# A fixed handicap for VectorE in the engine choice of a self-planning decoder kernel

## The chip, the cores and the metric

The kernel runs on one core of one Trainium2 chip. The metric is the time of one execution on the device in microseconds (us), the median of several runs. Engines are named as in the profile: PE is TensorE's matmul side and PEld its weight load, DVE is VectorE, ACT is ScalarE, POOL is GpSimd, and SP is SyncE, which here issues most of the transfers.

## The reference

Two layers of a decoder trunk, 512 tokens of 1024 features, all in float32. Cut to what matters here:

```
for l in range(2):
    u = rms_norm(x, norm_g[l]) * (1 + scale) + shift      # shift, scale, gate = silu(c) @ w_ada[l] + b_ada[l]
    z = u @ w_in[l]                                       # one wide projection, split into the parts below
    ya = dsa_attention(...)      # A: scores of an indexer, top 128 keys of each query, softmax over those
    yb = swa_sinks_attention(...)                         # B: window of 128 keys, with sinks
    yc = stick_breaking_attention(...)                    # C
    merged = sum(sigmoid(m_b) * ((y_b * silu(g_b)) @ w_br_b) for b in (a, b, c))
    x = x + gate * (merged @ w_out[l])
return rms_norm(x, final_g)
```

## The kernel before, in words

**Matmuls in three terms.** Every large product is made of two parts of each operand: a weight chunk that lands in `wstage` is cast to a short form `whi`, and `wlo = wstage - whi` is the rest; activations have `uh` and `ul` in the same way. A product is then `whi*uh + whi*ul + wlo*uh`, three matmuls of 128 x 512. So each chunk of weights (four blocks, 12 matmuls of PE) costs one cast and one subtraction on some other engine (`Chunks.do_split`). There are four buffers each of `wstage`, `whi` and `wlo`, three PSUM banks `ps_z` for projections and five `ps_s` for attention.

**Stages of a layer.** First seven column tiles of the projection that accumulate while the normed input is made (`first_phase`), then the value columns (`v_phase`, tiles of 364 columns). Then several streams are woven together: the indexer and its top-k, mixers C, B and A with four pairs of heads each, the other projection tiles, the branch products that are merged (`branch_item`: `xm <- ps_z, sm` and `sm <- ps_z, sm` take a branch product out of PSUM and multiply it by its gate), and in layer 1 the dot products with `w_ada` that layer 2 needs (`wstage <- wstage, csr`). Last comes the output product (`out_phase`). The top-k runs on VectorE alone: for each of three query blocks 16 times MAX8 and MATCH_REPLACE8 on `score`; mixer A cannot mask its logits before it is done. In mixer C the probabilities `t` are transposed by PE (`ps_s <- small, t`) and copied out to `U`; mixers A and B transpose through VectorE (`X <- X`) and DMA (`U <- X`, `V <- X`).

**A planner sets the order.** Nothing is issued as the Python code runs. `Recorder.add` records each operation with the engines that could do it (`alts`) and a cost on each. `cast` may go to ACT, DVE and, if the source is in SBUF, POOL; `both` (tensor-tensor operations) to POOL and DVE; `sq_` to three engines; a few more have two. `forward` then places one operation after another: for each engine it takes the ready operation that can start first, by urgency (`prio`, the latest start that `latest` found in the round before), and the earliest of the engines' candidates goes. Where an operation has several engines, `elsewhere` decides whether this engine must leave it: it compares when the operation would end here with when it would end on each other engine, from when that engine is free and from the cost there. `order` does five such rounds and keeps the one whose planned end is the earliest; `emit` writes it out. So one changed comparison can change every engine's order. `TOPORT` and `port` in the plan keep VectorE and GpSimd from using a shared SBUF port at once, and `emit` adds a dependency from the VectorE operation to the GpSimd operation that follows it there.

Of the kernel before, what the change touches and what calls it, by code (L numbers as in the profile page):

```python
# [25 lines left out]
F32 = mybir.dt.float32  # L26
F32R = mybir.dt.float32r
BF16 = mybir.dt.bfloat16
AF = mybir.ActivationFunctionType
# [4 lines left out]
P = 128  # L34
# [12 lines left out]
TR32 = {'a': (0, 1, 2, 3), 'b': (0, 1, 2, 3)}  # L47
# [34 lines left out]
class Weave:  # L82


    def __init__(self):
        self.items = []
        self.now = 0.0
        self.events = set()
# [193 lines left out]
class Recorder:  # L282
# [5 lines left out]
    ENTER = {"m": 0.0, "t": 0.035, "c": 0.17, "r": 0.17}  # L288
    TOPORT = 0.13
    ROUNDS = 5  # L290

    def __init__(self, tc, nc, psum, sbuf):
        self.tc, self.nc, self.psum, self.sbuf = tc, nc, psum, sbuf
# [263 lines left out]

    def elsewhere(self, x, name, at, E):

        end = at + x.alts[name].cost  # L560
        for o, y in x.alts.items():
            if o != name:
                t = max(E[o]["free"], x.est, x.soft.get(o, 0.0), E[o]["port"] if y.port else 0.0) + y.cost
                if t < end - 1e-9:
                    return True
        return False

# [28 lines left out]
    def order(self):  # L596
        best = None
        for n in range(self.ROUNDS):
            end, out = self.forward()
# [31 lines left out]
def op(cost, fn, *chunks):  # L631
    return ("op", cost, fn, [c + (phase[0],) for c in chunks])
# [15 lines left out]
def trunk(ctx, tc, xT, vecs, w_ss, w_gt, w_first, w_t, w_v, w_br, w_o, rope, consts, out):  # L648
# [7 lines left out]
    rec = Recorder(tc, nc, ps, sb)  # L656
    PE, ACT, DVE, POOL, SP = (rec.engine(e) for e in ("PE", "ACT", "DVE", "POOL", "SP"))
# [7 lines left out]
    def sbank():  # L665
        return rec.tile("ps_s", [P, S])
# [4 lines left out]
    def t512(tag, bufs=None, dt=F32):  # L671
        return rec.tile(tag, [P, S], dt)

    def mm(o, lhsT, rhs, start, stop=True):
        PE.matmul(o, lhsT, rhs, start=start, stop=stop, skip_group_check=True)
# [24 lines left out]
    def fill(out, v):  # L700
        rec.add({"POOL": ("memset", (out, v), {}), "DVE": ("memset", (out, v), {})})
# [9 lines left out]
    csb, o = small[:, 0:8], 8  # L711
    g_sb = [small[:, o + 8 * l:o + 8 * l + 8] for l in range(L)]
    fg_sb, o = small[:, o + 8 * L:o + 8 * L + 8], o + 8 * L + 8
    b_ada, o = [small[:, o + 24 * l:o + 24 * l + 24] for l in range(L)], o + 24 * L
    sink, o = small[:, o:o + 8 * L], o + 8 * L
# [59 lines left out]
    st = {}  # L775
# [403 lines left out]
    def low_parts(q, kl, pos, banks, b, p, order):  # L1179

        quads = []
        for e, i in order:
            k0, W = keys(b, i)
            bk, c0 = pos(e, i)
            hp = (H0, H1)[e]
            quads.append((banks[bk][:, c0:c0 + W], q[hp, e, 128 * i:128 * i + 128], kl[hp, k0:k0 + W], False))
        value_run(b, RIDE.get((b, p), ()), zbank, quads)
# [3 lines left out]
    def c_qk(p):  # L1191
        def fn():
            q = st[f"cq{p}"]
            kh, kl = st[f"ck{p}"]
            zb, pt = [None] * 5, [None] * 5
            for i in (3, 2, 0, 1):
                ts, W = slice(128 * i, 128 * i + 128), 128 * i + 128
                o, first = [None] * 2, [False] * 2
                for e in range(2):
                    bk, c0 = apos(e, i)  # L1200
                    if zb[bk] is None:
                        zb[bk], first[e] = sbank(), True
                    o[e] = zb[bk][:, c0:c0 + W]
                for e in range(2):
                    mm(o[e], q[:, e, ts], kh[:, e, :W], first[e])
                if i == 1:
                    mm(o[1], q[:, 1, ts], kl[:, S:], False)
            low_parts(q, kl, apos, zb, "c", p, LOW_ALL)
            for bk in (0, 3, 1, 4, 2):
                z = zb[bk]  # L1210
                if bk % 3:
                    m = z[:, 256:].rearrange("p (a b) -> p a b", a=2) if bk != 2 else z.rearrange("p (a b) -> p a b", a=2)[:, :, 128:]
                    DVE.tensor_tensor(out=m, in0=m, in1=cmask.unsqueeze(1).to_broadcast([P, 2, P]), op=OP.add)
                else:
                    DVE.tensor_tensor(out=z[:, 384:], in0=z[:, 384:], in1=cmask, op=OP.add)
                t = pt[bk] = t512("t", 10)
                u32 = mybir.dt.uint32
                rec.add({"ACT": ("activation", (t, z, AF.Abs), {}),
                         "DVE": ("tensor_scalar", (t.bitcast(u32), z.bitcast(u32), 0x7FFFFFFF, None), dict(op0=OP.bitwise_and))})
                ACT.activation(t, t, AF.Exp, scale=-1.0)  # L1220
                ACT.activation(t, t, AF.Ln, bias=1.0)
                DVE.scalar_tensor_tensor(t, z, 0.0, t, op0=OP.min, op1=OP.subtract)
                fill(t[:, 511:512], BIG)
                back = t[:, 0:511][:, ::-1]
                DVE.tensor_tensor_scan(back, z[:, 1:512][:, ::-1], back, BIG, op0=OP.add, op1=OP.subtract)
                ACT.activation(t, t, AF.Exp, scale=-1.0)
            st["p", p] = pt
        return op(2700, fn)

    def mixer_c():  # L1230
# [19 lines left out]
    def apos(e, i):  # L1250
        return ((1 + 3 * e, 384), (2, 256 * e), (1 + 3 * e, 0), (3 * e, 0))[i]
# [87 lines left out]
    def grid(X, b):  # L1339
        return X.split((4, blocks(b), 32), (1, 0, 2))  # L1340

    def strip(b, e, i):

        if b == "b":
            return (7 * e + 2 * i - 1, 1, 2) if i else (7 * e, 1, 1)
        return (i, 3, i + 1) if e == 0 else (16 + i, -4, i + 1)
# [4 lines left out]
    def strided(X, b, e, i):  # L1351
        g0, dg, n = strip(b, e, i)
        g = grid(X, b)
        return g[:, g0:(g0 + dg * n if g0 + dg * n >= 0 else None):dg]
# [450 lines left out]
```

## Time and profile before

| what | value |
|---|---|
| median of 3 runs | 1145.74 us (1144.85 to 1147.17) |
| the profiled execution's own time | 1142.08 us |
| its span, first to last instruction | 1140.3 us |
| PE busy | 1123.2 us (99%), 5619 matmuls |
| DVE busy | 984.5 us (86%), 2238 instructions |
| ACT busy | 530.2 us (46%), 1125 instructions |
| POOL busy | 169.4 us (15%), 237 instructions |
| weight casts `whi` of 128 x 512: DVE, ACT, POOL | 156, 103, 49 |

The profile shows one execution. Line 620 of the kernel is the one statement of `emit` that writes nearly every instruction, so groups have to be told apart by their tiles (`out <- in`), not by lines; line 618 is the same for some small matmuls. "Busy" is the union of an engine's intervals, the mean of a group is that of a single interval. Matmuls overlap: one of 128 x 512 has an interval of 0.39 us, but the next one starts 0.23 us after it where nothing holds it up. So an idle time that the trace shows on PE is about 0.16 us shorter than the time that PE lost there. Numbers in square brackets behind a row of the timeline are the engine's idle time before it and what ended it.

### The profile page before, as it was taken

How to read it: one execution, taken by the hardware profiler on the slowest of the kernel's cores; microseconds unless marked ns; L12 is line 12 of the kernel's file. 1: busy time of each engine (PE TensorE's matmuls, PEld its weight loads, DVE VectorE, ACT ScalarE, POOL GpSimd, SP SyncE). 2: the span in 40 equal slices, each digit the busy share in tenths (PEclk: the TensorE clock that was granted, in tenths of full speed). 3: DMA queues.
4: the chain of work that ended last, by engine and by line, in shares of the span. 5: the costliest groups of instructions: out<-in, count | busy, mean ns of one | idle time of the engine just before them, and what ended most of it. 6: DMA issues, size and time to landing. Idle time of an engine off the chain costs nothing.

```text
span 1140.3 us, 17580 instructions
## 1 busy us (share of the span) xinstructions
PE 1123.2 (99%) x5619; PEld 932.7 (82%) x5619; DVE 984.5 (86%) x2238; ACT 530.2 (46%) x1125; POOL 169.4 (15%) x237
## 2 busy tenths in 40 slices
PE   8999999999999999999999999999999999999997
PEld 6899878788887778788898998877888778877886
DVE  7977999999999987888686589999999999777765
ACT  5633767563446442433143247766435455433122
POOL 0100336310013200000000004551101221000001
PEclk9999999999999999999999999999999999999999
DMA  9744332445464573545634442234645455534343
GB/s 351 236 120 122 93 93 84 111 143 152 116 173 148 161 218 121 166 140 177 195 101 108 109 138 78 81 93 121 167 120 139 140 148 147 150 84 142 99 124 107
DMA packets 92764, 157.23 MB, mean 138 GB/s; under 512 B 14080, under 2 KB 28672, under 8 KB 92672
## 3 DMA queue, kind: packets, MB, share of 16 engines
q1 hardware_dynamic: 84608, 143.98, 43.2%
q10 hardware_dynamic: 8064, 12.13, 3.7%
q8 instruction: 44, 0.72, 0.3%
q14 instruction: 48, 0.39, 0.1%
HBM read 125.39 MB, written 4.19 MB: 114 GB/s over the span
## 4 chain that ended last, share of the span: by engine, by line
PE 82%; DVE 11%; DMA 2%; issue 2%; ACT 1%; SPq 0%; POOL 0%; DVEq 0%; ACTq 0%; POOLq 0%
PE ps_z L620 64%; PE ps_s L620 15%; DVE t L620 3%; PE ps_s L618 3%; DVE m L620 1%; DVE score L620 1%; DVE wlo L620 1%; PE ps_z L618 1%; DVE X L620 1%; DMA Y<-in_w_ss 1%; DVE zc L620 1%; DVE Y L620 1%; DVE e L620 0%; SPq L620 0%; DMA V<-X 0%
## 5 line engine op out<-in xcount | busy, mean ns | idle before, releaser
L620 PE MATMUL ps_z<-uh,whi 128*128 128x512 f32 (+1 forms) x905 | 354.1, 393 | 3.7 <-DVE sm L620 2.2
L620 PE MATMUL ps_z<-ul,whi 128*128 128x512 f32 (+1 forms) x905 | 353.1, 391 | 0.3 <-DVE ul L620 0.3
L620 PE MATMUL ps_z<-uh,wlo 128*128 128x512 f32 (+1 forms) x905 | 352.0, 390 | 0.0
L620 DVE TENSOR_TENSOR wlo<-wstage,whi 128x512 fp32r<-128x512 f32 (+2 forms) x322 | 210.8, 657 | 12.4 <-ACT whi L620 4.5
L620 PEld LDWEIGHTS ps_z<-uh,whi 128*128 128x128 f32 x905 | 170.2, 188 | 38.9 <-DVE sm L620 2.6
L620 PEld LDWEIGHTS ps_z<-ul,whi 128*128 128x128 f32 x905 | 170.3, 188 | 34.4 <-issue 1.2
L620 PEld LDWEIGHTS ps_z<-uh,wlo 128*128 128x128 f32 x905 | 170.3, 188 | 34.4 <-issue 0.2
L620 DVE CAST whi<-wstage 128x512 fp32r<-128x512 f32 (+1 forms) x200 | 81.0, 406 | 89.3 <-PE ps_z L620 72.7
L620 ACT CAST whi<-wstage 128x512 fp32r<-128x512 f32 (+2 forms) x122 | 73.0, 601 | 112.6 <-PE ps_z L620 67.7
L620 PE MATMUL ps_z<-Y,whi 128*128 128x512 f32 x384 | 118.5, 389 | 0.0
L620 ACT ACTIVATE e<-ps_z 128x512 f32<-128x512 f32 x68 | 40.4, 594 | 120.6 <-PE ps_z L620 89.4
L620 ACT ACTIVATE t<-t,nm 128x256 f32<-128x256 f32 (+3 forms) x128 | 65.2, 511 | 46.4 <-DVE nm L620 21.8
L620 POOL TENSOR_TENSOR wlo<-wstage,whi 128x512 fp32r<-128x512 f32 (+2 forms) x50 | 63.8, 1277 | 138.6 <-PE ps_z L620 52.3
L620 PEld LDWEIGHTS ps_z<-Y,whi 128*128 128x128 f32 x384 | 72.1, 188 | 15.0
L620 ACT ACTIVATE e<-e 128x512 f32<-128x512 f32 x96 | 59.8, 630 | 49.6 <-DVE e L620 47.2
L620 POOL CAST whi<-wstage 128x512 fp32r<-128x512 f32 (+1 forms) x50 | 30.6, 613 | 335.3 <-PE ps_z L620 236.9
L620 PE MATMUL ps_z<-Y,wlo 128*128 128x512 f32 x192 | 74.7, 389 | 0.0
L620 ACT ACTIVATE t<-t 128x512 f32<-128x512 f32 x120 | 67.0, 629 | 0.9
L620 DVE MAX8 m<-score 128x8 f32<-128x256 f32 (+2 forms) x96 | 53.2, 554 | 1.4
L620 PE MATMUL ps_s<-KH,Q 128*128 128x256 f32 (+3 forms) x280 | 50.9, 305 | 2.1 <-ACT U L620 0.9
L620 DVE MATCH_REPLACE8 score<-m,score 128x256 f32<-128x256 f32 (+2 forms) x96 | 52.0, 542 | 0.1
L620 PEld LDWEIGHTS ps_s<-KH,Q 128*128 128x128 f32 x280 | 42.5, 189 | 9.6 <-ACT U L620 1.8
(218 smaller groups left out, 1952.0 us busy)
## 6 DMA issues: line engine op xcount, KB each, us to landing
wstage<-in_w_t SPq DMA_DIRECT2D x212, 256.0 KB, 2.7
wstage<-in_w_v SPq DMA_DIRECT2D x48, 182.0 KB, 2.4
m<-zs SPq DMA_DIRECT2D x128, 64.0 KB, 2.0
wstage<-in_w_gt SPq DMA_DIRECT2D x32, 256.0 KB, 2.7
wstage<-in_w_ss SPq DMA_DIRECT2D x32, 256.0 KB, 2.8
wstage<-in_w_o SPq DMA_DIRECT2D x32, 256.0 KB, 2.7
Y<-in_w_ss SPq DMA_DIRECT2D x15, 512.0 KB, 5.6
wstage<-in_w_first SPq DMA_DIRECT2D x16, 256.0 KB, 3.2
```

The lines of the kernel that those rows point to most:

```text
L618: self.real[engine].matmul(*[real(a) for a in q[:3]], start=q[3], stop=True, skip_group_check=True)
L620: made = getattr(self.real[engine], y.op)(*[real(a) for a in y.args], **{k: real(v) for k, v in y.kw.items()})
```

## The change

`elsewhere` counts an operation on VectorE as ending 0.3 us later than its cost says (`FAVOUR`), on both sides of the comparison: VectorE leaves an operation to another engine even if that ends it up to 0.3 us later, and another engine leaves it to VectorE only if VectorE would be over 0.3 us earlier. The costs and the times in the plan itself are as they were.

```
+    FAVOUR = 0.3
...
     def elsewhere(self, x, name, at, E):

-        end = at + x.alts[name].cost
+        end = at + x.alts[name].cost + (self.FAVOUR if name == "DVE" else 0.0)
         for o, y in x.alts.items():
             if o != name:
                 t = max(E[o]["free"], x.est, x.soft.get(o, 0.0), E[o]["port"] if y.port else 0.0) + y.cost
-                if t < end - 1e-9:
+                if t + (self.FAVOUR if o == "DVE" else 0.0) < end - 1e-9:
                     return True
         return False
```

The diff has a second part in `c_qk`, for the case that mixer C's pairs are listed in `TR32`. They are not (`TR32` has only `'a'` and `'b'`), so mixer C does what it did.

Counted over the whole order, VectorE's `whi` casts go from 200 to 36, ScalarE's from 122 to 231 and GpSimd's from 50 to 105; `wlo` subtractions of 128 x 512 go from 261 to 244 on VectorE and from 47 to 64 on GpSimd. Of the smaller movements, VectorE gives up all 25 casts of `Q`, `KH` that are 64 x 512 and come from SBUF, 10 of 14 copies to `U`, and 14 of the 25 operations that split `Y` (8 subtractions, 6 casts). PE has the same matmuls in another order.

The first place is VectorE near the start of the program, from the sums over `w_ada` (`Y`) to the first normed input (`V`, which makes the first `uh`). Before:

```order
L620 SCALAR_TENSOR_TENSOR Y,dot<-Y,csr 128x512 x2
L620 CAST whi<-wstage 128x512
L620 TENSOR_TENSOR dot<-dot 128x1
L620 CAST whi<-wstage 128x384
L620 TENSOR_SCALAR amul_78<-dot,small,gb 128x1
L620 TENSOR_TENSOR wlo<-wstage,whi 128x512
L620 TENSOR_TENSOR V_104<-V_104,ps_s 128x256 x2
```

The same place now:

```order
L621 SCALAR_TENSOR_TENSOR Y,dot<-Y,csr 128x512 x2
L621 TENSOR_TENSOR dot<-dot 128x1
L621 CAST whi<-wstage 128x384
L621 TENSOR_SCALAR amul_78<-dot,small,gb 128x1
L621 TENSOR_TENSOR wlo<-wstage,whi 128x384
L621 TENSOR_TENSOR wlo<-wstage,whi 128x512
L621 SCALAR_TENSOR_TENSOR Y,dot<-Y,csr 128x1024
L621 TENSOR_TENSOR V_104<-V_104,ps_s 128x256 x2
```

One cast has left for ScalarE, and one subtraction and one sum over `Y` have come in ahead of `V`.

The second place is VectorE in layer 1, in the top-k of the third query block (`score_1242`, 128 x 512), which mixer A waits for. Before, from its ninth to its tenth round:

```order
L620 MAX m_3377<-score_1242 128x8
L620 TENSOR_SCALAR X<-t,den 128x2x4x32
L620 TENSOR_TENSOR wlo<-wstage,whi 128x512
L620 TENSOR_TENSOR zc<-ps_z,rt 128x512
L620 TENSOR_SCALAR X<-t,den 128x2x4x32
L620 MATCH_REPLACE score_1242<-m_3377,score_1242 128x512
L620 CAST whi<-wstage 128x512
L620 TENSOR_TENSOR den<-den,mx 128x4
L620 SCALAR_TENSOR_TENSOR wstage,dotg<-wstage,csr 128x512
L620 TENSOR_TENSOR wlo<-wstage,whi 128x512
L620 RECIPROCAL den<-den 128x4
L620 MAX m_3436<-score_1242 128x8
```

The same block now:

```order
L621 TENSOR_TENSOR xm_3163<-ps_z,sm 128x512
L621 MATCH_REPLACE score_1242<-m_3158,score_1242 128x512
L621 TENSOR_SCALAR mods_76<-dotg,small 128x1
L621 MAX m_3177<-score_1242 128x8
L621 MATCH_REPLACE score_1242<-m_3177,score_1242 128x512
L621 MAX m_3191<-score_1242 128x8
L621 MATCH_REPLACE score_1242<-m_3191,score_1242 128x512
L621 MAX m_3202<-score_1242 128x8
L621 MATCH_REPLACE score_1242<-m_3202,score_1242 128x512
```

Mixer B's work stood between the rounds; now they follow each other during mixer C's merge. After the eighth merge product of the layer 11 MAX8 and 12 MATCH_REPLACE8 of the block were left, and now 2 and 3 are.

The third place is PE in layer 1 at the end of mixer C: its last transposes (`small,t`), projection tiles (`uh`, `ul`), the first matmuls of mixer B (`KH,Q`, which need an attention bank) and mixer C's value products (`U,V`). Before:

```order
L620 MATMUL ps_s<-small,t 128x128 x4
L620 MATMUL ps_z<-uh_329,wlo 128x512
L620 MATMUL ps_z<-uh_373,whi 128x512
L620 MATMUL ps_z<-ul_395,whi 128x512
L620 MATMUL ps_z<-uh_373,wlo 128x512
L620 MATMUL ps_z<-uh_431,whi 128x512
L620 MATMUL ps_s<-KH,Q 128x256 x9
L618 MATMUL ps_s<-U,V_671 64x512 x2
```

The same place now, with 18 of the projection matmuls and the narrower value products left out:

```order
L621 MATMUL ps_s<-small,t 128x128 x4
L621 MATMUL ps_z<-ul_494,whi 128x512
...
L619 MATMUL ps_s<-U,V_674 64x512 x2
...
L621 MATMUL ps_z<-uh_372,wlo 128x512
L621 MATMUL ps_s<-KH,Q 128x256 x12
```

There were 5 projection matmuls between the last transposes and mixer B's first matmul; there are 20 now, and the value products.

More of the change, by code (lines that the diff above doesn't have):

```diff
@@ L290 @@
     ROUNDS = 5
+    FAVOUR = 0.3
     def __init__(self, tc, nc, psum, sbuf):
@@ L558, in elsewhere @@
     def elsewhere(self, x, name, at, E):
-        end = at + x.alts[name].cost
+        end = at + x.alts[name].cost + (self.FAVOUR if name == "DVE" else 0.0)
         for o, y in x.alts.items():
@@ L563, in elsewhere @@
                 t = max(E[o]["free"], x.est, x.soft.get(o, 0.0), E[o]["port"] if y.port else 0.0) + y.cost
-                if t < end - 1e-9:
+                if t + (self.FAVOUR if o == "DVE" else 0.0) < end - 1e-9:
                     return True
@@ L1194, in fn @@
             kh, kl = st[f"ck{p}"]
-            zb, pt = [None] * 5, [None] * 5
+            zb, pt, X = [None] * 5, [None] * 5, None
             for i in (3, 2, 0, 1):
@@ L1225, in fn @@
                 DVE.tensor_tensor_scan(back, z[:, 1:512][:, ::-1], back, BIG, op0=OP.add, op1=OP.subtract)
-                ACT.activation(t, t, AF.Exp, scale=-1.0)
-            st["p", p] = pt
+                if p not in TR32.get("c", ()):
+                    ACT.activation(t, t, AF.Exp, scale=-1.0)
+                    continue
+                if X is None:
+                    X = rec.tile("X", [P, 20 * P], F32)
+                for e in range(2):
+                    for i in range(4):
+                        b_, c0 = apos(e, i)
+                        if b_ == bk:
+                            W = 128 * i + 128
+                            ACT.activation(strided(X, "c", e, i), t[:, c0:c0 + W].split((W // P, 4, 32), (0, 1, 2)), AF.Exp, scale=-1.0)
+            st["p", p] = X or pt
         return op(2700, fn)
```

## The prediction

> **What bounds the kernel now.** I read the page first, then the busy time by stretches, then PE's own rows where it waits.
>
> ```profile
> span 1140.3 us, 17580 instructions
> PE 1123.2 (99%) x5619; PEld 932.7 (82%) x5619; DVE 984.5 (86%) x2238; ACT 530.2 (46%) x1125; POOL 169.4 (15%) x237
> PE 82%; DVE 11%; DMA 2%; issue 2%; ACT 1%; SPq 0%; POOL 0%; DVEq 0%; ACTq 0%; POOLq 0%
> ```
>
> PE is the bound: busy for 99% of the span, and 82% of the chain that ended last. The change takes no matmul away, so it can win only where PE waits. Those places show in the timeline of PE as a row with idle time before it, here with two undisturbed rows first.
>
> ```profile
> 331.05 0.39 PE L620 MATMUL ps_z<-uh,whi 128*128 128x512 f32 x1
> 331.28 0.39 PE L620 MATMUL ps_z<-ul,whi 128*128 128x512 f32 x1
> ...
> 214.06 1.30 PE L620 MATMUL ps_s<-KH,Q 128*128 128x256 f32 x7 [0.46 <-ACT U L620]
> ...
> 333.29 0.70 PE L620 MATMUL ps_s<-KH,Q 128*128 128x512 f32 x3 [0.49 <-DVE KH L620]
> ...
> 362.86 0.50 PE L620 MATMUL ps_z<-uh,whi 128*128 128x512 f32 x1 [1.56 <-DVE zc L620]
> ...
> 418.06 0.50 PE L620 MATMUL ps_z<-uh,whi 128*128 128x512 f32 x1 [2.18 <-DVE sm L620]
> ...
> 775.24 0.99 PE L620 MATMUL ps_s<-KH,Q 128*128 128x256 f32 x6 [0.43 <-ACT U L620]
> ...
> 906.82 0.50 PE L620 MATMUL ps_s<-KH,Q 128*128 128x384 f32 x2 [0.51 <-DVE e L620]
> ```
>
> Undisturbed, matmuls start 331.28 - 331.05 = 0.23 us apart though each shows 0.39, so a wait costs its idle time plus 0.16. That makes 0.62 us at 214, 0.65 at 333, 1.72 at 363, 2.34 at 418, 0.59 at 775 and 0.67 at 907, four of the six ended by DVE and the other two by a copy to `U`. Four lie in layer 1 and two in layer 2. Busy time by stretch says why (columns: stretch, length, then PE, PEld, DVE, ACT, POOL, each with its count, then granted clock, DMA share, GB/s).
>
> ```profile
> 187.00:215.00 28.00, 27.54 (x146) 21.58 (x144) 27.53 (x53) 18.84 (x37) 15.75 (x21) 1.00 0.37 99
> 285.50:417.40 131.90, 128.15 (x618) 102.91 (x614) 127.86 (x333) 69.28 (x172) 19.75 (x22) 1.00 0.55 158
> 845.70:969.40 123.70, 123.19 (x610) 100.43 (x607) 119.90 (x301) 63.83 (x152) 23.01 (x24) 1.00 0.50 139
> 418.00:422.00 4.00, 3.94 (x10) 3.11 (x11) 3.82 (x9) 0.00 (x0) 0.00 (x0) 0.57 0.78 224
> ```
>
> The second row runs from the eighth to the eleventh merge product of layer 1, the third over the same work of layer 2. In layer 1 DVE is busy 127.86 of 131.90 us and ACT only 69.28: DVE is as full as PE there and runs late. In layer 2, without the `w_ada` products, it has 119.90 us of work and PE hardly waits.
>
> The fourth row holds a second cost of the wait at 418. The granted clock falls to 0.57, and 10 matmuls start in 4.00 us where 4.00 / 0.23 = 17.4 would: 7.4 x 0.23 = 1.7 us. The 1.56 us of idle time at 363 brought none of this (its stretch has clock 1.00). The Trainium skill (TensorE: Matmul & The Clock Gate, Part 1) has the clock fall after a whole idle window of some 3.4 us; the trace has it after 2.18 us, so the measurement decides. By the page's rule those 1.7 us would not belong to the wait, and the forecast would come out 1.7 us higher.
>
> **What leaves DVE and where it goes.** The prices:
>
> ```profile
> L620 DVE CAST whi<-wstage 128x512 fp32r<-128x512 f32 x156 | 65.7, 422 | 60.7 <-PE ps_z L620 53.9 <-PE ps_s L620 6.5
> L620 DVE CAST whi<-wstage 128x364 fp32r<-128x364 f32 x38 | 13.2, 348 | 27.0 <-PE ps_z L620 17.2 <-PE ps_s L620 9.7
> L620 ACT CAST whi<-wstage 128x512 fp32r<-128x512 f32 x103 | 63.8, 619 | 101.3 <-PE ps_z L620 67.1 <-DMA V<-X 16.4 <-issue 5.2
> L620 POOL CAST whi<-wstage 128x512 fp32r<-128x512 f32 x49 | 30.1, 615 | 318.0 <-PE ps_z L620 236.9 <-DVE den L620 30.7 <-DVE score L620 15.1
> L620 DVE TENSOR_TENSOR wlo<-wstage,whi 128x512 fp32r<-128x512 f32 x261 | 178.2, 684 | 10.4 <-ACT whi L620 4.5 <-POOL whi L620 1.1 <-DVE whi L620 0.5
> L620 POOL TENSOR_TENSOR wlo<-wstage,whi 128x512 fp32r<-128x512 f32 x47 | 60.9, 1295 | 73.9 <-DVE whi L620 37.0 <-ACT whi L620 18.8 <-DVE Y L620 7.5
> L620 DVE MAX8 m<-score 128x8 f32<-128x512 f32 x32 | 21.9, 683 | 0.2
> L620 DVE MATCH_REPLACE8 score<-m,score 128x512 f32<-128x512 f32 x32 | 21.6, 675 | 0.0
> ```
>
> By the orders DVE loses 125 casts of 512 columns (52.8 us at 422 ns), 34 of 364 (11.8) and 17 subtractions (11.6); the other 25 casts, copies and scalings that leave bring it to an estimated 105 us in all, 984 to about 880. ACT takes 80 casts of 512 (49.5 us at 619 ns) and the rest of what moved, some 80 us. Its fullest quoted stretch, 18.84 of 28.00 us, is two thirds; by the order some 3 us of work are added there, so ACT does not become the bound. POOL takes 45 casts (27.7 us at 615 ns), 17 subtractions (22.0 at 1295 ns) and smaller pieces, again some 80 us.
>
> *Layer 1, mixers B and A* (the waits at 333 and 363). In the stretch 285.5 to 417.4 the new order has 9 MAX8 and 9 MATCH_REPLACE8 fewer, which now stand earlier, where casts made room: 9 x (0.683 + 0.675) = 12.2 us. The rest of the stretch balances to about 3 us less. DVE's 127.86 us become some 113, against 131.90 - 0.65 - 1.72 = 129.5 us that PE needs: 87%. Layer 2's stretch had 119.90 of 123.70, 97%, and only the 0.67 us wait. So 2.37 us of waits should shrink to about 0.3: gain **2.1**, between 0 and 2.4.
>
> *The wait at 418.* It has a nearer cause than the average:
>
> ```profile
> 415.14 2.29 DVE L620 STREAM_TRANSPOSE X<-X 128x640 f32<-128x640 f32 x3
> 417.36 0.65 DVE L620 TENSOR_TENSOR sm<-ps_z,sm 128x512 f32<-128x512 f32 x1
> ```
>
> `sm`, which frees PE's bank, is queued on DVE behind three transposes of mixer A. The new order keeps these three ahead of it, and between the tenth and the eleventh merge product it has 33 rows of DVE where there were 28. Only the backlog that DVE brings into that piece shrinks. I expect half of the wait, 1.2 us, to stay; that is less than the 1.56 us that cost no clock, so the 1.7 us go whole. Gain 2.34 - 1.2 + 1.7 = **2.8**, between 0 (all stays) and 4.0 (all goes).
>
> *Layer 2's wait at 907* falls with 15 us of DVE work gone from its stretch too: gain **0.5** of 0.67. *The two waits for `U`* (0.62 and 0.59): PE had 5 matmuls between its last transposes and the first `KH,Q`, 5 x 0.23 = 1.2 us for the copy that frees the bank; now it has 20 and the value products, over 4.6 us. Gain **1.2**.
>
> *The start* gets worse.
>
> ```profile
> 13.92 0.42 DVE L620 CAST whi<-wstage 128x512 fp32r<-128x512 f32 x1
> 14.26 0.15 DVE L620 TENSOR_TENSOR dot<-dot 128x1 f32<-128x1 f32 x1
> ...
> 15.38 1.33 DVE L620 TENSOR_TENSOR V<-V,ps_s 128x256 f32<-128x256 f32 x3
> ...
> 17.63 1.21 DVE L620 SCALAR_TENSOR_TENSOR Y<-Y,csr 128x1024 f32<-128x1024 f32 x1
> 18.77 0.07 DVE L620 DVE_READ_ACCUMULATOR Y<-Y,csr 128x1 f32 x1
> ...
> 16.48 0.51 PE L620 MATMUL ps_z<-uh,whi 128*128 128x256 f32 x2
> ...
> 20.38 0.51 PE L620 MATMUL ps_z<-ul,whi 128*128 128x256 f32 x2 [0.29 <-DVE ul L620]
> ...
> L620 DVE TENSOR_TENSOR wlo<-wstage,whi 128x384 fp32r<-128x384 f32 x15 | 8.2, 547 | 0.3
> ```
>
> Ahead of `V` one cast goes (14.26 - 13.92 = 0.34 us from start to start) and a 384-column subtraction (0.547, less the 0.08 by which neighbours overlap: 0.47) and a sum over `Y` (18.77 - 17.63 = 1.14) come in: `V`, `uh` and PE's first real matmul come 1.27 us later than 16.48. The wait of 0.45 at 20.38 is then absorbed, since DVE makes its `ul` before PE gets there. Loss **0.8**, between 0 (if the plan's sum over `Y` fills a time in which `V` would wait for ACT) and 1.3.
>
> *New waits.* The longer casts and POOL's subtractions are prepared several chunks ahead, and 12 matmuls x 0.23 = 2.8 us of PE per chunk cover 0.619 + 0.684. The trace has no PE wait for POOL, so I bound this by 0 below and take one wait of the size at 214, **0.6**, with rival 3 as the upper side. The end of the program keeps its pieces: 0.
>
> **Sum:** 2.1 + 2.8 + 0.5 + 1.2 - 0.8 - 0.6 = 5.2 us. The profiled execution took 1142.08 us, 1.8 more than its span, and so would come to 1136.9. It is 3.7 below the median of the runs, 1145.74; carried over to that, the forecast is **1140.5**. About 0.2% (2.3 us, as much as the three runs spread) is what a measurement here can tell from no change.
>
> **The rivals.**
>
> 1. *The waits only move.* DVE's piece before `sm` is no lighter, so the wait at 418 stays with its clock loss and the start costs all of 1.3 us: 2.1 + 0.5 + 1.2 - 1.3 - 0.6 = 1.9, **1143.8**. For it: the three transposes are still there. Against: DVE arrives with 15 us less behind it. Chance 0.14.
>
> 2. *The relief is eaten by the port that DVE and POOL share.* If every added 80 us of POOL holds up DVE's subtractions, only 25 of 105 us of relief are left, a quarter of the four gains: (2.1 + 2.8 + 0.5 + 1.2) / 4 - 0.8 - 0.6 = 0.2, **1145.5**. For it: DVE's `wlo` reach 0.868 us at the longest. Against: their mean is 0.684, so few ever meet POOL in the plan of before.
>
> ```profile
> L620 DVE TENSOR_TENSOR wlo<-wstage,whi x322: 527/681/868, 14.8 to 1120.7; 128x512 fp32r<-128x512 f32 x131, 128x364 fp32r<-128x364 f32 x23, 128x384 fp32r<-128x384 f32 x7
> ```
>
> The Trainium skill (SBUF — State Buffer, "SBUF: two separate sides") speaks for this rival: it calls that pair of ports an exclusive lock, held for a whole instruction. By that rule the time is this rival's. The trace shows it little, hence chance 0.10.
>
> 3. *Slower: low halves come late from POOL.* Each of the 17 subtractions that POOL takes over ends 1.295 - 0.684 = 0.61 us later. If PE had to wait for each, 10.4 us are lost: 6.6 - 0.8 - 10.4 = -4.6, **1150.3**. It decides from 10 of the 17 on (5.8 / 0.61). Against: 47 such ran before and none of the quoted waits is POOL's; for: POOL's rows come closer together now. Chance 0.12.
>
> 4. *The planner falls back on nearly the old order.* The order shows otherwise: 36 casts on DVE in place of 200. 1145.7, chance 0.02.
>
> **How the numbers follow.** The forecast has 0.62. Nearly all of it and a third of rival 1 are faster by over 0.2%: 0.65. Rival 2, rival 4, the rest of rival 1 and the forecast's tail are within: 0.23. Rival 3 is slower: 0.12. The low end is every wait gone and nothing new, 2.4 + 4.0 + 0.7 + 1.2 = 8.3, and 1 us of the runs' spread: 1136.4. The high end takes in rivals 1, 2 and 4 and their spread, 1147.0, and leaves out rival 3.
>
> **What would show it.** Right: DVE near 880 us busy, PE's matmuls unchanged; no wait of 0.4 us or more for `U`, `KH` or `zc`; at `sm` in layer 1 under 1.6 us idle and a clock of 1.00 throughout after the start; PE's first `uh,whi` near 17.7 us. Wrong: a clock loss still at `sm` (rival 1); DVE's `wlo` mean well above 0.684 (rival 2); PE rows with waits ended by POOL `wlo` (rival 3); a new wait of over 2 us anywhere, which none of the terms has.

## The result

| | before | after |
|---|---|---|
| median of the runs made together | 1145.30 us (1143.06 to 1147.17) | 1138.51 us (1137.93 to 1139.06) |
| the profiled execution, its span | 1142.08, 1140.3 us | 1139.06, 1137.3 us |

The ratio is 0.9941, with a 95% interval of 0.9923 to 0.996: 6.8 us faster, where 5.2 were forecast. The two profiled executions lie only 3.0 us apart; the difference is taken up below.

### The profile after

The page of the changed kernel: span, busy time, and the chain that ended last by engine.

```profile
span 1137.3 us, 17668 instructions
PE 1121.5 (99%) x5619; PEld 932.1 (82%) x5619; DVE 897.1 (79%) x1960; ACT 619.0 (54%) x1299; POOL 256.0 (23%) x341
PE 93%; DVE 3%; DMA 2%; issue 1%; SPq 0%; ACT 0%; POOL 0%; DVEq 0%; POOLq 0%
```

DVE lost 87.4 us, ACT and POOL gained 88.8 and 86.6. PE's share of the chain rose from 82% to 93%, DVE's fell from 11% to 3%. Next the waits of PE from 57 us (the value phase of layer 1) to 1125 us, first before, then after (us in all, times, the longest).

```profile
PE ps_z L620 <- DVE sm L620: 2.2, 1, 2.2
PE ps_z L620 <- DVE zc L620: 1.6, 1, 1.6
PE ps_s L620 <- ACT U L620: 0.9, 2, 0.5
PE ps_s L620 <- DVE e L620: 0.5, 1, 0.5
PE ps_s L620 <- DVE KH L620: 0.5, 1, 0.5
PE ps_s L620 <- DVE mx L620: 0.2, 1, 0.2
```

```profile
PE ps_z L619 <- DMA m<-zs: 3.4, 1, 3.4
```

Every wait that the prediction priced is gone, and there is one that it did not have. It stands at 376.18 us, where PE starts mixer A's first value product. PE's row there, and the first projection matmul:

```profile
17.83 0.51 PE L621 MATMUL ps_z<-uh,whi 128*128 128x256 f32 x2
...
376.18 4.54 PE L619 MATMUL ps_z<-U,va 128*64 128x512 f32 x16 [3.40 <-DMA m<-zs]
```

The row names `m<-zs` as the last to come, but the product reads `U`, and by the trace the last of its sixteen transfers `U<-X` lands at 376.09. The two long stretches of before, at the same times in the changed kernel, and four of 3.41 us around the new wait (length, PE, PEld, DVE, ACT, POOL, clock, DMA share, GB/s):

```profile
285.50:417.40 131.90, 128.50 (x617) 103.97 (x614) 115.17 (x296) 74.65 (x183) 26.78 (x29) 0.97 0.54 157
845.70:969.40 123.70, 123.59 (x601) 101.44 (x600) 105.17 (x252) 75.56 (x185) 29.07 (x34) 1.00 0.50 141
...
371.20:374.61 3.41, 1.58 (x11) 1.00 (x9) 0.58 (x3) 0.00 (x1) 0.00 (x0) 1.00 0.55 134
374.61:378.03 3.42, 1.85 (x6) 0.71 (x8) 2.56 (x5) 2.50 (x5) 0.00 (x0) 0.50 0.59 145
378.03:381.44 3.41, 3.41 (x16) 1.93 (x13) 2.07 (x4) 1.72 (x3) 1.16 (x2) 0.50 0.85 299
381.44:384.85 3.41, 3.41 (x16) 2.81 (x16) 3.35 (x10) 2.27 (x4) 1.32 (x2) 1.00 0.02 6
```

In the first two DVE has 12.7 and 14.7 us less to do, so it is 87% and 85% busy there. (Cut by the same merge products instead, at 285.6 to 418.9 and 843.6 to 966.8, DVE is busy for 116.6 of 133.3 and 105.0 of 123.2 us, the same shares.) In the last four the clock is halved for 6.8 us behind the wait; PE is busy for 1.85 + 3.41 us of it and loses half of that, 2.6 us. With 3.4 us of idle time the new wait costs 6.0 us.

Where it comes from shows on ACT's queue, and in the transfers of that place (count, KB each, median us from issue to landing), after and then before:

```profile
364.61 9.90 ACTq L621 DMA_DIRECT2D U<-X  x9
374.61 0.62 ACT L621 CAST whi<-wstage 128x512 fp32r<-128x512 f32 x1 [10.40 <-DMA U<-X]
...
U<-X ACTq DMA_DIRECT2D x9, 80.0 KB, 4.2
U<-X SPq DMA_DIRECT2D x7, 80.0 KB, 3.3
wstage<-in_w_ss SPq DMA_DIRECT2D x1, 256.0 KB, 6.1
```

```profile
369.68 5.47 ACTq L620 DMA_DIRECT2D U<-X  x8
...
U<-X ACTq DMA_DIRECT2D x8, 80.0 KB, 2.5
U<-X SPq DMA_DIRECT2D x8, 80.0 KB, 2.6
```

Before, ACT issued its eight of the sixteen transfers in 5.5 us, and they landed in 2.5 us (median). Now its nine take 9.9 us to issue, and one up to 6.05 to land. By the trace three loads of 256 KB were issued on SP at 363.60, 364.22 and 364.72, directly ahead of them; and an issue goes out each time just after an older transfer has landed (at 369.33, 370.32, 370.80 and 371.40, after landings at 369.31, 370.30, 370.78 and 371.39), when eight are in flight. So late landings hold up the later issues, and ACT, in whose queue half of them stand, does no copy for 10.4 us.

### The profile page after: what moved, and what is told of

Its sections match the earlier page's. It is cut to its first block, busy times and chain, and to the rows that moved or that the text cites. A ratio compares the mean times of both kernels' runs of the same rounds, so it can differ in the third digit from the quotient of the medians.

```text
span 1137.3 us, 17668 instructions
## 1 busy us (share of the span) xinstructions
PE 1121.5 (99%) x5619; PEld 932.1 (82%) x5619; DVE 897.1 (79%) x1960; ACT 619.0 (54%) x1299; POOL 256.0 (23%) x341
## 4 chain that ended last, share of the span: by engine, by line
PE 93%; DVE 3%; DMA 2%; issue 1%; SPq 0%; ACT 0%; POOL 0%; DVEq 0%; POOLq 0%
PE ps_z L621 72%; PE ps_s L621 16%; PE ps_s L619 3%; PE ps_z L619 2%; DMA Y<-in_w_ss 1%; DMA wstage<-in_w_ss 1%; SPq L621 0%; DVE Y L621 0%; DVE wlo L621 0%; DMA m<-zs 0%; DVE t L621 0%; DMA U<-X 0%; DVE Q L621 0%; DVE zc L621 0%; DVE klow L621 0%
## 5 line engine op out<-in xcount | busy, mean ns | idle before, releaser
L621 DVE TENSOR_TENSOR wlo<-wstage,whi 128x512 fp32r<-128x512 f32 (+2 forms) x306 | 204.4, 670 | 124.9 <-ACT whi L621 104.5
L621 ACT CAST whi<-wstage 128x512 fp32r<-128x512 f32 (+2 forms) x231 | 137.1, 594 | 251.7 <-PE ps_z L621 156.5
L621 POOL CAST whi<-wstage 128x512 fp32r<-128x512 f32 (+2 forms) x105 | 64.1, 611 | 454.3 <-PE ps_z L621 283.4
L621 POOL TENSOR_TENSOR wlo<-wstage,whi 128x512 fp32r<-128x512 f32 (+1 forms) x66 | 84.8, 1287 | 110.1 <-DVE ul L621 56.9
L621 PE MATMUL ps_s<-KH,Q 128*128 128x256 f32 (+3 forms) x280 | 47.9, 302 | 0.0
L621 PE MATMUL ps_s<-whi,uh 128*128 128x364 f32 x144 | 47.8, 332 | 0.0
L621 PE MATMUL ps_s<-wlo,uh 128*128 128x364 f32 x144 | 47.4, 329 | 0.0
L621 PE MATMUL ps_s<-whi,ul 128*128 128x364 f32 x144 | 47.1, 329 | 0.0
```

Source lines behind the costliest of these rows:

```text
L621: made = getattr(self.real[engine], y.op)(*[real(a) for a in y.args], **{k: real(v) for k, v in y.kw.items()})
```

## The experiments

**Theory:** the gain is the relief of DVE (its copies come in time, so PE's waits for DVE vanish); part of it is given back by the later start and by the collision at 376. **Rivals:** the gain is the other order, which any disturbance of the planner could draw; POOL's work is paid back on the shared port; the wait at 376 is an accident of one execution. All kernels compute the same. The times stand beside runs of the kernel before on the same chip; DVE's busy time and PE's waits are read in the views shown above, the waits from 57 to 1125 us.

| run | DVE busy | PE waits for DVE | for others | median, us | ratio, 95% interval |
|---|---|---|---|---|---|
| before | 984.5 | 5.0 | 0.9 | | |
| e9, before again | 985.0 | 6.0 | 1.0 | 1144.29 (one) | |
| e4, handicap 0.02 | 982.3 | 6.7 | 1.7 | 1144.93 | 1.0004 (0.9994 to 1.0014) |
| e5, handicap 0.1 | 980.3 | 2.1 | 2.2 | 1140.10 | 0.9974 (0.9964 to 0.9983) |
| e12, casts only | 922.7 | 2.6 | 7.3 | 1148.02 | 1.0034 (1.0021 to 1.0046) |
| e6, POOL favoured | 915.9 | 1.3 | 11.6 | 1147.77 | 1.0042 (1.0027 to 1.0056) |
| after | 897.1 | 0 | 3.4 | 1138.51 | 0.9941 (0.9923 to 0.996) |
| e10, after again | 898.0 | 0 | 2.0 | 1137.89 | 0.9936 (0.9924 to 0.9949) |
| e3, loads behind | 896.8 | 0 | 2.4 | 1136.60 | 0.9932 (0.9919 to 0.9945) |
| e8, loads and sum behind | 897.8 | 0 | 2.1 | 1135.77 | 0.9937 (0.9925 to 0.9949) |
| e11, ACT held in the plan | 900.6 | 0 | 0.7 | 1135.80 | 0.9918 (0.9906 to 0.993) |
| e7, handicap 0.6 | 819.6 | 2.1 | 1.7 | 1144.21 | 1.0009 (1.0001 to 1.0017) |

### Order and engines taken apart (e1, e2)

Both plans are made, one with FAVOUR 0 and one with 0.3; the sequence is taken from one of them and each instruction's engine from the other.

```
+        for self.FAVOUR in (0.0, 0.3):
...
+            plans.append(self.plan())          # the old order()
+        seq, other = plans[0], plans[1]        # e2: plans[1], plans[0]
+        where = {x.i: e for x, e in other[1]}
...
+        return [(x, where[x.i]) for x, e in seq[1]]
```

> Every instruction stands where the order of before has it, but runs on the engine that the plan with the handicap gave it. Theory (the gain is relief of DVE): DVE near 900 us busy; the waits of PE that DVE ended at 333, 363, 418 and 907 shrink from 5.4 us to under 2, the clock loss at 418 goes, the two waits for U stay; 1139 to 1142 us. Rival (the gain is the other order, the relief is worth nothing): 1144.5 to 1146, with the same waits. A second rival (casts moved into an order that was not planned for them come late): new waits ended by ACT or POOL casts, over 1147.

> The reverse: the order of the plan with the handicap, each instruction on the engine of before. Theory: DVE near 984 us busy again, PE waits for DVE come back at places of their own, 1142 to 1148 us. Rival (the order is the gain): 1137.5 to 1140, as with the whole change.

Measured: 1179.18 and 1178.14 us, ratios 1.03 (1.0283 to 1.0317) and 1.0296 (1.028 to 1.0311). Only the second rival of e1 had this, and nothing had it for e2. In e1 new waits come from every engine; the longest is 5.2 us for a `KH` cast that now stands on POOL. The test is inconclusive for its question: both mixtures lose some 34 us, many times what was to be split, since the sequence of one plan does not fit the engines of the other.

### Disturbed, but not relieved (e4, e5)

```
-    FAVOUR = 0.3
+    FAVOUR = 0.02      # e5: 0.1
```

> A handicap of 0.02 us in place of 0.3: DVE keeps its casts (201 in place of 200 before), but the planner's choices are disturbed and its order is another. Theory (relief of DVE): 1144 to 1147 us, DVE near 984 busy. Rival (any disturbance of the planner moves the time by several us, and the change only drew a good one): more than 3 us away from 1145.3 on either side.

> A handicap of 0.1 us: again another order, with VectorE still doing 195 of its 200 casts. Theory (relief of DVE): DVE near 984 us busy, waits of PE for DVE in the two layers of over 4 us in all, 1143 to 1147 us. Rival (the order drawn decides): under 1141 or over 1149.

e4 is as expected by the theory: another order, DVE as full as before, the same time. e5 is not. It gains 3.2 us, about half of what the change does, with DVE at 980.3 us. Its longest waits:

```profile
PE ps_z L621 <- DVE sm L621: 1.6, 2, 1.3
PE ps_s L621 <- ACT KH L621: 1.4, 2, 1.0
PE ps_z L619 <- DMA U<-X: 0.8, 1, 0.8
```

Waits for DVE remain (2.1 us with two short ones left out here), but no single long one, and the clock does not fall in the layers. So the largest item of the prediction, the wait at 418 with its clock loss, can go by another order with hardly any relief. The theory in its plain form fell here.

### Relieved in other ways (e6, e7, e12)

```
-        end = at + x.alts[name].cost + (self.FAVOUR if name == "DVE" else 0.0)
+        end = at + x.alts[name].cost + (self.FAVOUR if name in ("DVE", "ACT") else 0.0)   # e6, and so in the other line
...
-    FAVOUR = 0.3
+    FAVOUR = 0.6                                                                            # e7
...
+                h = self.FAVOUR if x.alts[name].op in ("tensor_copy", "copy") else 0.0      # e12, h in place of FAVOUR
```

> The handicap of 0.3 us on VectorE and ScalarE alike, so that GpSimd is what takes over: 212 of the 372 casts on GpSimd, 108 on ScalarE, 52 on VectorE. Theory (what counts is that DVE has room, whoever takes the work): DVE 880 to 930 busy, PE's waits for DVE in the layers under 2 us in all, 1136 to 1141 us. Rival (DVE and POOL share a port, so POOL's work is paid back): mean of DVE's 128x512 subtraction wlo well above 0.68 (0.75 or more), 1143 to 1147 us.

> Twice the handicap, 0.6 us: no cast left on VectorE, and 172 of 372 subtractions on GpSimd in place of 66. Theory: with 0.3 PE's waits for DVE are gone already, so there is no more to gain; GpSimd's subtractions of 1.29 us now come late, PE shows waits ended by POOL wlo, 1140 to 1150 us. Rival (the more relief the better): under 1137 us.

> The handicap of 0.3 us for casts and copies alone; subtractions and sums are chosen as before. Theory (relief of DVE by the casts is the main thing): DVE 900 to 930 us busy, PE's waits for DVE under 2 us in all, 1136 to 1141 us. Rival (the subtractions that went to GpSimd are needed as well): waits for DVE over 4 us, 1142 to 1146.

None of the three is faster than before. e6 and e12 have what the theory asked for, DVE at 916 and 923 us, and waits for DVE of 1.3 and 2.6 us (under 2 was expected). What they lose is something else; the longest waits of e6, then ACT ahead of the first of them, then the longest of e12:

```profile
PE ps_s L621 <- ACT KH L621: 6.5, 2, 6.1
PE ps_z L619 <- DMA m<-zs: 3.0, 2, 2.0
PE ps_s L619 <- DMA U<-X: 2.1, 1, 2.1
...
332.95 5.83 ACTq L621 DMA_DIRECT2D V<-X  x5
338.82 0.62 ACT L621 CAST KH<-zc 64x512 fp32r<-64x512 f32 x1 [7.16 <-DMA V<-X]
```

```profile
PE ps_z L620 <- DMA U<-X: 5.2, 2, 4.4
PE ps_s L622 <- ACT KH L622: 1.7, 1, 1.7
PE ps_s L622 <- DVE e L622: 1.4, 1, 1.4
```

It is the wait of 376 again, in other places: in e6 the `KH` cast that PE needs stands on ACT behind five `V<-X` whose issue takes 5.83 us; in e12 `U` itself lands late. By the traces loads of 256 KB stand there too: in e6 three, issued on SP at 331.88, 332.50 and 332.99, ahead of the `V<-X`; in e12 two, at 371.58 and 372.27, ahead of the last five `U<-X` of ACT. With the halved clock behind them (two stretches of e6, one of e12) the waits for others than DVE cost an estimated 16 us in e6 (11.6 and 4.3 of clock) and 10 in e12 (7.3 and 2.8).

The port rival misses in e6: DVE's 128x512 `wlo` take 701 ns there, not 750. The mean does grow with POOL's busy time, 684 ns at 169 us, 699 at 256, 701 at 346, and in e7, with 444 us on POOL, 744:

```profile
L621 DVE TENSOR_TENSOR wlo<-wstage,whi 128x512 fp32r<-128x512 f32 x193 | 143.6, 744 | 103.6 <-ACT whi L621 77.3 <-POOL whi L621 25.5
```

By the traces the growth sits in the few that meet POOL. In the changed kernel 225 of the 244 are overlapped for no more than 0.05 us by a cast or tensor-tensor operation of POOL and take 684 ns in the mean; the 11 that overlap a tensor-tensor operation of POOL take 1003, up to 1526. In e7 those are 20, with a mean of 1148, and the 158 undisturbed ones take 688.

The time of e7 was as expected, but not for the reason: PE shows no wait for POOL's `wlo`. By the trace it loses most at the starts of the two layers, where PE waits for `uh` from ACT: the value phase of layer 1 begins at 59.09 us in place of 56.19, and from the last output products of layer 1 to the value phase of layer 2 another 2.1 us are lost (54.1 us in place of 52.0).

### The wait at 376 (e3, e8, e10, e11)

e3 and e8 change nothing in the plan; they move instructions in the finished sequence of the changed kernel (numbers are those of the recorded list: 3185 and 3205 load `in_w_t` and `in_w_ss`, 3035 is the last `U<-X` on SP, 3278 the sum that reads `in_w_ss`).

```
+        # e3: behind 3035: loads 3185, 3205
+        # e8: 3185 behind 3035; 3205 behind 3156 (m<-zs); 3278, 3279, 3280 behind 3091 (e<-ps_z,G)
+        late = [q for q in seq if q[0].i in some]
+        seq = [q for q in seq if q[0].i not in some]
+        seq = seq[:at] + late + seq[at:]
```

> The changed kernel, with two weight loads of 256 KB (one in_w_t, one in_w_ss) issued on SP behind the sixteen U<-X transfers of mixer A's first pair of layer 1 instead of ahead of them. Theory (these transfers collided with the loads, which made PE wait 3.4 us at 376 and cost another 3.4 us of clock): the U<-X land in 2.2 to 3 us each, the wait at 376 is under 0.5 us, the clock stays 1.00, 1131.5 to 1134 us. Rival (the transfers are slow by themselves, or start too late because DVE's transposes do): the wait stays over 2 us and the time at 1138 to 1139.5.

> The changed kernel with the two weight loads behind the U<-X as in e3, and the in_w_ss load with the sum that reads it (on DVE) moved back further, behind the gate product e of that place. Theory: in e3 the rest of the wait at 375 came from U<-X still queued with those loads, and the wait at 380 from DVE standing 3.8 us in front of that sum; both shrink, 1.1 and 1.6 us to under 0.6 and 0.8, and the time is 1134 to 1136. Rival (the sum was not what held DVE): the wait at 380 stays at 1.5 us or more, 1136 to 1138.

The waits and ACT's issue of `U<-X` in e3, then in e8 (which has 0.3 us for ACT's `e` besides):

```profile
PE ps_z L623 <- ACT KH L623: 1.4, 1, 1.4
PE ps_z L621 <- DMA m<-zs: 1.0, 1, 1.0
...
364.91 6.62 ACTq L623 DMA_DIRECT2D U<-X  x9
```

```profile
PE ps_z L625 <- DMA m<-zs: 1.2, 2, 1.0
PE ps_z L627 <- ACT KH L627: 0.6, 1, 0.6
...
364.70 6.55 ACTq L627 DMA_DIRECT2D U<-X  x9
```

With two of the three loads out of the way ACT issues its nine in 6.6 us (9.9 above), the transfers land in 2.9 and 2.7 us in e3 (4.2 and 3.3 above), the wait falls from 3.4 to 1.0 and the clock stays up there. So the loads lengthen the wait, but they are not all of it. The moved work then made a wait of its own at 380 (1.4 us), which the second edit cut to 0.6, as expected; the first wait did not fall further, which was not. The spans of the profiled executions, 1134.5 and 1133.8 us, are 2.8 and 3.5 us below the 1137.3 of after, less than the 4.5 us and more that were expected of e3. Of the ratios neither differs from that of the change by more than the intervals, so that the edits save time is not shown.

> The changed kernel once more. Theory: 1137 to 1139.5 us, with the wait for U at 376 and its clock loss again (they come from the order of the transfers, not from chance). Rival (the wait at 376 was an accident of one execution): it is gone or under 1 us, and the time is under 1136.

```profile
PE ps_z L619 <- DMA m<-zs: 2.0, 1, 2.0
...
366.25 8.27 ACTq L621 DMA_DIRECT2D U<-X  x9
```

The wait is there again, 2.0 us long with one halved window behind it, so it belongs to the order; its length varies. The medians of the landing times, 2.9 us for ACT's transfers and 2.4 for SP's, are here no longer than in e3, although the loads stand ahead; what sets the two executions with the loads ahead apart from e3 and e8 is the longest landing (6.05 and 5.10 us against 3.74 and 3.37), ACT's issue (9.90 and 8.27 against 6.62 and 6.55) and the wait (3.4 and 2.0 against 1.0 and 1.0). These are two executions on each side, and by them the two loads account for 1.0 to 2.4 us of idle time.

e11 changes one condition in the plan, so that ACT too has to wait in it where eight transfers are in flight, and plans again:

```
-                if name == "SP" and len(lanes) >= self.LANES:
+                if name in ("SP", "ACT") and len(lanes) >= self.LANES:
```

> The change, and the plan also holds ScalarE, not only SP, at a transfer when eight are in flight (in the traces an issue on either follows the landing of the eighth before it within 0.02 us). Theory (the plan put casts on ScalarE behind transfers whose waiting it did not see): PE's waits that end by a DMA or by ACT shrink from 4.8 us plus 2.7 of clock to under 4 in all, those for DVE stay near 1, 1133 to 1137 us. Rival (it only draws another order): 1137 to 1142.

```profile
PE ps_z L619 <- DMA m<-zs: 0.5, 1, 0.5
...
363.12 5.02 ACTq L621 DMA_DIRECT2D U<-X  x8
```

Hardly a wait is left (0.2 us for a cast of ACT besides), and ACT's transfers are issued in 5.02 us. Ratio 0.9918: faster than before, and 2.1 us below e10 in the same comparison, though the intervals of the two overlap. It is one draw of the planner, so whether the new condition or another order did it is not settled; whether it would also have mended e6 and e12 was not tried.

### Before once more (e9)

> The kernel before once more, unchanged, for a second profile: the profile shown had 1142.08 us, 3.7 below the median of its runs. If its executions differ by how long the start takes, the first projection matmul or the value phase comes up to 2 us later here and all later places keep that distance; if they differ in the middle, other waits than those at 214, 333, 363, 418, 775 and 907 us appear.

```profile
PE ps_z L620 <- DVE sm L620: 3.0, 1, 3.0
...
PE ps_s L620 <- DVE e L620: 1.2, 1, 1.2
```

The span is 2.2 us longer than in the first profile: 0.6 at the start, 0.8 more at `sm` and 0.7 more at `e`. The waits for a full DVE vary from execution to execution, and the profile that the prediction used had short ones. That accounts for 2.2 of the 3.8 us by which the two spans lie closer together (3.0) than the medians (6.8); e9 and e10 differ by 5.9 (1144.29 and 1138.42).

## Why the prediction came out right, step by step

**The mixers of layer 1, the wait at 907, the two for `U`: right.** DVE's work in the stretch 285.5 to 417.4 was put at 113 us and is 115.17 (116.6 between the same merge products); the waits at 333 and 363 are gone (2.4 us, 2.1 forecast), those at 907 and for `U` too (0.67 and 1.2; 0.5 and 1.2).

**The wait at 418: gone, but not for the reason given.** The prediction had half of it stay, because, as it says of the three transposes in front of `sm`, "The new order keeps these three ahead of it". They are still ahead, and `sm` is nearly as late as it was. DVE, ACT and PE of the changed kernel there:

```profile
416.65 2.29 DVE L621 STREAM_TRANSPOSE X<-X 128x640 f32<-128x640 f32 x3
418.86 0.65 DVE L621 TENSOR_TENSOR sm<-ps_z,sm 128x512 f32<-128x512 f32 x1
...
416.72 0.60 ACT L621 ACTIVATE e<-ps_z 128x512 f32<-128x512 f32 x1
...
418.19 0.39 PE L621 MATMUL ps_z<-uh,whi 128*128 128x512 f32 x1
```

ACT of the kernel before, at the same step:

```profile
416.01 6.94 ACTq L620 DMA_DIRECT2D U<-X  x9
423.00 0.60 ACT L620 ACTIVATE e<-ps_z 128x512 f32<-128x512 f32 x1 [7.11 <-DMA U<-X]
```

`sm` starts 8.67 us after its branch product ended (410.19), before it was 9.64 (407.72). But PE goes on at 418.19 without it. Of the three `ps_z` banks the next projection tile now takes the one that ACT's copy `e` frees at 416.72 + 0.60 = 417.32; before, that copy stood behind nine `U<-X` in ACT's queue until 423.00, so PE had to wait for DVE's bank. The whole 4.0 us came back (the upper end of that term), through the order on ACT and not through a lighter DVE. e5, with a full DVE and no such wait, fits this. The clock part of the term was tied to the length of the wait (1.2 us is less than the 1.56 that cost none); by the grid shown at the end the place of a wait counts as well, so that half of it could still have cost the 1.7 us.

**The start: right for the profiled execution, with a part left out.** The first projection matmul was put 1.27 us later and is 1.35 later; by the value phase 0.54 is left (0.8 forecast). But the wait for `V` in front of it has grown to 1.91 us, and in e3, e10 and e11 it fell so that the clock was halved behind it; there the value phase starts at 57.8 to 58.3 us, while it is 56.7 in after and 57.1 in e8. The term had no clock in it.

**New waits: mis-sized.** 0.6 us were put in, bounded by waits for POOL. They cost 6.0 us, and came from transfers. The text had named what would show it wrong, "a new wait of over 2 us anywhere, which none of the terms has", and that is what the profile shows. The size could have been bounded from the trace of before, where ACT stands still for 7.11 us behind `U<-X`: a step that moves 80 us of copies onto ACT has to be weighed against the transfers in ACT's own queue, not only against its busy time.

**DVE's own time: off by 18 us.** It was to fall by 105 us to near 880 and fell by 87.4 to 897.1. The casts that left were priced by their intervals (0.42 us), but each overlaps its neighbour by about 0.08, as the prediction itself says at the start (0.34 from start to start). The intervals of DVE's groups sum up to 110 us less; with 278 instructions fewer some 278 x 0.08 = 22 us of that are overlap, an estimate that gives the 88 us seen.

**The sum.** The waits removed are worth 2.4 + 4.0 + 0.7 + 1.2 = 8.3 us, the best case of the prediction; less 0.5 at the start and 6.0 at 376 this leaves 1.8 of the 3.0 us between the two spans. Where the other 1.2 us came from was not traced. The forecast was near by luck in part, because two errors met: the wait at 418 gave 1.2 us more, the new wait took 5.4 more. Part of the gap between the medians (6.8) and the spans (3.0) is the spread of executions. Of the signs that were named, the first projection matmul (17.83), the matmuls and the wait at `sm` came as said; the full clock after the start and no wait of 0.4 us for `U` did not.

**The rivals.** Waits for POOL's `wlo` (rival 3) did not come. The shared port (rival 2) shows as 699 - 684 = 15 ns on the mean of 244 subtractions, 3.7 us of DVE and not 80: those that meet a tensor-tensor operation of POOL are long, but they are 11. The waits did not merely move (rival 1) on DVE; a new one came on a resource that no rival had. What the relieved kernels add: the five executions with DVE near 900 us show no wait for DVE, but four of them have one order, but for the moved instructions, so these are two draws. e6, e12 and e7, with DVE at 916, 923 and 820 us, still wait 1.3, 2.6 and 2.1 us for it, where e5 with a full DVE waits 2.1. That the waits for DVE went, and what that was worth, is shown; that a lighter DVE and not the order drawn with it removed them is argued, and only in part borne out: of the four executions with a full DVE three (before, e9, e4) wait 5.0 to 6.7 us. And where the drawn order puts loads among `U<-X` or `V<-X`, or copies behind them, more is lost than the relief brings.

## What to carry to other kernels

When work moves to an engine that also issues transfers, look at what stands in that engine's queue behind them: its busy share (54% here) says nothing of the 10 us in which it only issued. With a planner in the loop one change of a rule is one draw: run neighbours of it (another size of the rule, another way to the same relief) before the gain is put down to the rule. And compare the median of several executions, since one profile of a kernel with a full engine can lie 3 us to the side.

## What the runs showed of the hardware

**The clock is decided on a grid of 3.41 us.** In the ten profiles with more than one fall of the clock, all falls of one execution start a whole number of 3.413 us apart (210.00 of them between 418.47 and 1135.27 us before, 222.00 between 374.61 and 1132.37 after), and in the layers the clock stays down for 3.41 or 6.83 us. On that grid of the kernel before, two pairs of windows:

```profile
360.44:363.86 3.42, 1.86 (x8) 1.24 (x7) 3.42 (x9) 3.42 (x14) 1.27 (x1) 1.00 0.90 285
363.86:367.27 3.41, 3.41 (x16) 2.80 (x15) 3.29 (x10) 3.28 (x9) 0.00 (x0) 1.00 0.61 166
415.06:418.47 3.41, 1.23 (x6) 0.72 (x5) 3.41 (x7) 0.80 (x2) 0.00 (x0) 1.00 0.74 222
418.47:421.88 3.41, 3.41 (x10) 2.63 (x9) 3.35 (x8) 0.00 (x0) 0.00 (x0) 0.50 0.79 229
```

PE busy for 1.86 of 3.42 us (54%) was followed by full clock, 1.23 of 3.41 (36%) by half; after has 1.58 (46%) followed by half. Over all profiles a fall from full clock had a window at most 52% busy ahead of it, and below 42% it always came; between the two it came after some windows and not after others. So a wait of 2 us costs 1.7 us more or nothing, by where it falls on the grid: the wait of 1.9 us for `V` was followed by half clock in three of the six executions that have it. The Trainium skill (TensorE: Matmul & The Clock Gate, Part 1) has a free-running window of 4096 cycles at 1.2 GHz, 3413 ns, which agrees with the grid; that it takes a whole idle window these runs don't bear out.

**Transfers beside loads.** A `U<-X` of 80 KB landed in 2.5 us (median) in the kernel before. Directly behind three loads of 256 KB, issued within 1.2 us, it took up to 6.05 us (5.10 in e10), and up to 3.74 and 3.37 us with two of the loads moved (e3, e8). The issuing engine was held with it: ACT's nine took 9.90 and 8.27 us to issue behind the loads, 6.62 and 6.55 without the two.

**DVE beside POOL.** Of DVE's 128x512 subtractions the 11 that overlap a tensor-tensor operation of POOL took 1003 ns in the mean, the 225 undisturbed ones 684 (the changed kernel).
